# Recurrent mixer of a streaming encoder: gates and convolution weights moved ahead of the receptances, later weight splits moved behind the inverses

## The chip, the cores and the metric

The kernel runs on one core of a Trainium2 chip. The metric is the time of one execution on the device in microseconds. The core's engines are TensorE (PE in the profile: matmuls; its weight loads are PEld), VectorE (DVE), ScalarE (ACT), GpSimd (POOL) and SyncE (SP), which here only starts transfers. Each engine takes its instructions in the order in which they were written into its queue; the queues run side by side and wait for one another by semaphores. DMA transfers are started from SyncE's and ScalarE's queues.

## The reference

Two layers act on a float32 stream x of 256 positions by 1024 channels. Each is a feed-forward network, a mixer and a second feed-forward network, each between two RMS norms. The first layer's mixer is the recurrent one, which the change touches; the second layer's is attention. The recurrent mixer, cut to what matters:

```
proj = h @ w_in                                   # columns: r, k, v, lora (decay, rate, gate), c_val, c_gate
p = p + shift_mu * (previous position of p - p)   # for the recurrent columns
kk = normalised k * k_k;   a = sigmoid(...);   k = k * (1 + (a - 1) * k_a)
# for each of 8 heads of 64 channels, over the positions t:
S_t = S_{t-1} diag(w_t) - (S_{t-1} kk_t)(kk_t * a_t)^T + v_t k_t^T
y_t = S_t r_t
bonus = sum(r * k * r_k) * v                      # over the channels of a head
y_a = (group_norm(y) * lnx_g + lnx_b + bonus) * g
glu = c_val * sigmoid(c_gate)
y_b = silu(layer_norm(conv over 31 positions of glu))
out = concat(y_a, y_b) @ w_out
```

## The kernel before

**Stages.** The kernel runs six stages one after the other: feed-forward 0, recurrent mixer A, feed-forward 1, feed-forward 3, attention mixer C, feed-forward 4. Mixer A takes the stretch from about 207 to 396 us of the span.

**Weights.** Weights come from DRAM in pages of 128 x 1024 fp32, 512 KB each, in one planned list. `Stream.load` starts their loads on SyncE's queue as buffers (`raw`) come free. A page is split before its use: ScalarE casts a high part `whi`, VectorE (for some pages GpSimd) subtracts it and gets the low part `wlo`; TensorE then makes three products (high by high, low by high, high by low). The splits are `split`, line 102 for the cast and 104 for the difference. `upto` splits pages up to a given key. The convolution's pages (`acw`) are used as they come, without a split. Keys: `alora`, `av`, `ak`, `ar` for lora, values, keys and receptances, `acv` and `acg` for the gate values and the gates of the convolution, `ao` for the output.

**Steps of mixer A.** The string `ORDER` names the steps in the order in which they are written out, one letter each. Q (`qmats`) makes for each chunk of 64 positions and each head the matrix that has to be inverted. I (`invert`) writes Q to DRAM (`dq`), reads its 16 x 16 diagonal blocks back (`inv<-dq`), inverts them on VectorE in a chain of small products and sums (lines 774 to 798), writes the inverses to DRAM twice, plain (`dg`) and transposed (`dt`), and reads them back as diagonal blocks of `G` and `T`. R (`receptance`) makes r and its scaled form in `ur`. C (`glu`) makes the gated values of the convolution and shifts them by one position with transfers. A (`amats`) makes the scores of keys and receptances (`ak`, `ar`) in four chunks of 8 products. B (`kback`) transposes keys back and c (`conv`) starts the convolution. 2 (`doubling`) grows the 16 x 16 inverses to 64 x 64 with products of `T`, `Q`, `G` and `WT`. b (`bonus`) makes the bonus on GpSimd. S (`state`) walks the four chunks: Q times G, then `vz`, then the state `SB`. `weigh` makes the weights of the bonus from r times k, 16 small matmuls.

**Taps.** The convolution's 31 taps by channel group are spread as filler: some as scaled additions on VectorE (`feed`, in amounts `FEED`), the others as matmuls on TensorE (`pfeed`, in amounts `PFEED`), 8 taps for each `acw` page. In the trace one fp32 matmul of these is two records.

**What sets the order.** The steps are written in the order of `ORDER`; `issue_after(x)` asks that an instruction be put behind x in the engine's queue.

The four writes of `dq` in `invert`, half on each queue:

```
for t in range(2):
    (nc.scalar, nc.sync)[t].dma_start(out=rows64(dq, c)[:, t], in_=Q[zs, t])
```

## Time and profile before

| | us |
|---|---|
| median of 3 runs | 1115.91 (1115.58 to 1116.05) |
| the profiled execution | 1117.59 |
| its span, first to last instruction | 1115.6 |
| TensorE busy | 1083.3 (97%) |
| VectorE busy | 644.4 (58%) |
| ScalarE busy | 545.0 (49%) |
| GpSimd busy | 208.9 (19%) |
| mean granted clock of TensorE | 0.987 |

The profile is of one execution, taken by the hardware profiler; its times are microseconds from the start of the span. The granted clock is the share of full speed that TensorE had. An engine that is not busy waits, and the trace names what ended the wait. Busy time of TensorE includes time at the lower clock, in which the same work takes twice as long.

### The profile page before, as it was taken

Reading aid. Unit: us, or ns where it says so; the run is one execution under the profiler, and the core shown is the slowest. Engines: PE = TensorE matmul, PEld = TensorE weight load, DVE = VectorE, ACT = ScalarE, POOL = GpSimd, SP = SyncE. Lnnn points to the kernel's source line nnn. Section 1 sums busy time; section 2 is a strip of 40 time slices with the busy share of each in tenths; the row PEclk is TensorE's granted clock in tenths of the full one; section 3 lists DMA queues with packets and bytes.
Section 4 is the critical chain, followed back from the end, with each engine's and each line's share of the span. In section 5 each row is a group of like instructions: output and inputs, shape, how many; then the busy total and the mean of one; then the engine's idle time right before and its main releaser. Section 6 shows DMA issues by size and latency. Waiting matters only on the chain.

```text
span 1115.6 us, 17671 instructions
## 1 busy us (share of the span) xinstructions
PE 1083.3 (97%) x7021; PEld 951.6 (85%) x7021; DVE 644.4 (58%) x1050; ACT 545.0 (49%) x876; POOL 208.9 (19%) x155
## 2 busy tenths in 40 slices
PE   7999999999799999999999999999999999999997
PEld 5899998879688789999888999988787778999986
DVE  4565662578755556557545555836657655555822
ACT  7444544574111574446354544635666855444611
POOL 5200004334030160000034000001555423000000
PEclk9999999999699999999999999999999999999999
DMA  9765785246621138655635454744273555665400
GB/s 356 253 215 183 239 292 150 82 157 189 152 86 58 43 147 281 229 174 208 222 116 209 167 188 177 271 159 150 78 273 124 159 177 180 219 181 193 140 1 38
DMA packets 66632, 192.84 MB, mean 173 GB/s; under 512 B 18520, under 2 KB 20216, under 8 KB 66550
## 3 DMA queue, kind: packets, MB, share of 16 engines
q1 hardware_dynamic: 56698, 189.75, 50.2%
q10 hardware_dynamic: 9852, 1.96, 1.0%
q8 instruction: 55, 0.90, 0.3%
q14 instruction: 27, 0.22, 0.1%
HBM read 187.86 MB, written 2.92 MB: 171 GB/s over the span
## 4 chain that ended last, share of the span: by engine, by line
PE 85%; DVE 5%; ACT 4%; issue 2%; DMA 2%; POOL 1%; ACTq 0%; SPq 0%; DVEq 0%; POOLq 0%
PE gu L361 31%; PE acc L270 21%; PE gu L230 15%; PE acc L600 5%; PE gu L347 4%; PE acc L372 3%; PE gu L600 1%; ACT whi L102 1%; DVE wlo L104 1%; DMA inv<-dq 1%; POOL misc L118 1%; POOL p L496 1%; PE tr L250 1%; PE tr L163 1%; DMA raw<-in_wgt_dram 1%
## 5 line engine op out<-in xcount | busy, mean ns | idle before, releaser
L102 ACT CAST whi<-raw 128x1024 fp32r<-128x1024 f32 x294 | 301.7, 1047 | 212.5 <-PE gu L361 93.2
L104 DVE TENSOR_TENSOR wlo<-raw,whi 128x1024 fp32r<-128x1024 f32 x256 | 317.3, 1248 | 150.5 <-ACT whi L102 125.9
L361 PE MATMUL gu<-xth,whi 128*128 128x256 f32 x1104 | 312.7, 283 | 1.4 <-ACT xth L167 1.4
L361 PE MATMUL gu<-xth,wlo 128*128 128x256 f32 x1104 | 312.8, 284 | 0.0
L361 PE MATMUL gu<-xl,whi 128*128 128x256 f32 x1104 | 312.2, 283 | 0.0
L361 PEld LDWEIGHTS gu<-xth,whi 128*128 128x128 f32 x1104 | 211.5, 192 | 5.0 <-ACT xth L167 2.0
L361 PEld LDWEIGHTS gu<-xth,wlo 128*128 128x128 f32 x1104 | 211.6, 192 | 2.6 <-issue 0.3
L361 PEld LDWEIGHTS gu<-xl,whi 128*128 128x128 f32 x1104 | 211.3, 192 | 1.2 <-issue 1.0
L270 PE MATMUL acc<-whi,ht 128*128 128x512 f32 x576 | 168.2, 393 | 0.0
L118 POOL TENSOR_TENSOR misc<-misc 128x1 f32<-128x1 f32 (+1 forms) x36 | 32.3, 898 | 496.5 <-DVE misc L135 377.4
L104 POOL TENSOR_TENSOR wlo<-raw,whi 128x1024 fp32r<-128x1024 f32 x38 | 92.2, 2459 | 157.3 <-PE acc L270 140.6
L270 PEld LDWEIGHTS acc<-whi,ht 128*128 128x128 f32 x576 | 103.9, 189 | 18.2
L270 PE MATMUL acc<-wlo,ht 128*128 128x512 f32 x288 | 89.9, 392 | 0.0
L241 DVE TENSOR_TENSOR h<-gu,h 128x256 f32<-128x256 f32 x88 | 36.8, 419 | 75.5 <-ACT h L237 71.9
L230 PE MATMUL gu<-whi,xth 128*128 128x512 f32 x160 | 63.1, 400 | 2.5 <-ACT whi L102 1.5
L270 PEld LDWEIGHTS acc<-wlo,ht 128*128 128x128 f32 x288 | 53.9, 188 | 11.8
L230 PE MATMUL gu<-wlo,xth 128*128 128x512 f32 x160 | 63.3, 397 | 0.5 <-DVE wlo L104 0.5
L230 PE MATMUL gu<-whi,xl 128*128 128x512 f32 x160 | 63.5, 400 | 0.0
L239 DVE TENSOR_TENSOR h<-gu,misc 128x256 f32<-128x256 f32 x56 | 23.7, 423 | 65.2 <-PE gu L361 65.1
L237 ACT ACTIVATE h<-gu,misc 128x256 f32<-128x256 f32 x32 | 15.1, 474 | 76.1 <-PE gu L230 42.3
L104 POOL TENSOR_TENSOR flo<-raw,fhi 128x1024 fp32r<-128x1024 f32 x8 | 19.0, 2389 | 149.8 <-ACT fhi L102 149.4
L347 PE MATMUL gu<-whi,xth 128*128 128x512 f32 x112 | 44.7, 399 | 1.6 <-ACT v L435 1.6
(259 smaller groups left out, 1528.5 us busy)
## 6 DMA issues: line engine op xcount, KB each, us to landing
raw<-in_wgc_dram SPq DMA_DIRECT2D x112, 512.0 KB, 4.7
raw<-in_wd_dram SPq DMA_DIRECT2D x88, 512.0 KB, 5.0
raw<-in_wgt_dram SPq DMA_DIRECT2D x64, 512.0 KB, 5.5
raw<-in_cin_dram SPq DMA_DIRECT2D x24, 512.0 KB, 4.9
raw<-in_ain_dram SPq DMA_DIRECT2D x18, 512.0 KB, 4.7
raw<-in_aout_dram SPq DMA_DIRECT2D x8, 512.0 KB, 5.8
raw<-in_cgate_dram SPq DMA_DIRECT2D x8, 512.0 KB, 4.5
raw<-in_cout_dram SPq DMA_DIRECT2D x8, 512.0 KB, 5.0
```

Source lines behind the costliest of these rows:

```text
L102: self.nc.scalar.copy(out=hi, in_=raw)
L104: (engine or self.nc.vector).tensor_tensor(out=lo, in0=raw, in1=hi.bitcast(F32), op=ALU.subtract)
L118: self.pow = self.nc.gpsimd.tensor_tensor(out=out, in0=v, in1=self.mhalf[:, :n], op=ALU.pow)
L230: nc.tensor.matmul(ps, lhsT=l, rhs=r[:, k % 2], start=n == 0, stop=n == 23)
L237: nc.scalar.activation(sl, ps[:, 0:256], AF.Silu, scale=rstd[u[2]])
L239: nc.vector.tensor_tensor(out=z, in0=ps[:, 0:256], in1=self.rb, op=ALU.mult)
L241: nc.vector.tensor_tensor(out=h, in0=ps[:, 256:512], in1=sl, op=ALU.mult)
L270: mm = nc.tensor.matmul(out, lhsT=l, rhs=r, start=u[1] == 0 and i + n == 0, stop=u[1] == NB - 1 and i * 3 + n == 5)
L347: self.nc.tensor.matmul(ps, lhsT=l, rhs=r[:, k % 2], start=n == 0, stop=n == 23)
L361: self.nc.tensor.matmul(ps[:, j * 256:(j + 1) * 256], lhsT=l, rhs=r, start=n == 0, stop=n == 23)
L372: yield lambda acc, l=l, r=r, c=c, first=k == ks[0] and n == 0, last=k == ks[7] and n == 2: self.nc.tensor.matmul(acc[c], lhsT=l, rhs=r[:, ...
L600: return nc.tensor.matmul(out, lhsT=lhsT, rhs=rhs, start=start, stop=stop, skip_group_check=True)
```

## The change

The change does these things in mixer A:

- Gates and gate values (C) and the convolution's start (c) are written ahead of the receptances (R); R now makes r times k itself. The weighing matmuls, and a new step p (`ahead`) with the first taps, stand ahead of the scores, and two taps behind each chunk of them. `PFEED` is 16, 2, 2, 6.
- The `acw` pages are loaded ahead of the `ao` pages. The first `ao` load stands behind the first gate shift, the later ones behind the loads of `G` and `T`.
- All four writes of `dq` go through ScalarE's queue; the write of `dg` goes through SyncE's, that of `dt` stays on ScalarE's. The constants of the inverse and its products share one buffer.
- The splits of `ao` and of the next stage are held behind the last `G` of the doubling (`m["doubled"]`) and the last copy of `kback`.
- The norm's gain page (`ln`) takes the buffer of k and is loaded through ScalarE's queue; the output's gain page (`gp`) is fetched 7 weight loads behind and not 14.

```diff
-ORDER = "VLDKPvQskRICABc2bS"
+ORDER = "VLDKPvQskICcRpAB2bS"
...
-FEED, PFEED = (3, 2, 6), (14, 2, 8)
+FEED, PFEED = (3, 2, 6), (16, 2, 2, 6)
...
-                    (nc.scalar, nc.sync)[t].dma_start(out=rows64(dq, c)[:, t], in_=Q[zs, t])
+                    nc.scalar.dma_start(out=rows64(dq, c)[:, t], in_=Q[zs, t])
...
-            for src, dd, dst in ((TI, dt, T), (GV, dg, G)):
-                nc.scalar.dma_start(out=diag(dd), in_=src)
+            for src, dd, dst, queue in ((TI, dt, T, nc.scalar), (GV, dg, G, nc.sync)):
+                queue.dma_start(out=diag(dd), in_=src)
                 for zs, c in halves:
                     for t in range(2):
-                        (nc.scalar, nc.sync)[t].dma_start(out=dst[zs, t], in_=rows64(dd, c)[:, t])
+                        i = (nc.scalar, nc.sync)[t].dma_start(out=dst[zs, t], in_=rows64(dd, c)[:, t])
+
+            W.gates[W.where["ao", 0][1] + 1] = i
...
+            V.tensor_tensor(out=r, in0=r, in1=k, op=ALU.mult)
+
         def weigh(behind):
             rk = grp(m["r"])
+            psb = self.bank("tr", 2)
             with self.tc.issue_after(behind.ins):
-                V.tensor_tensor(out=rk, in0=rk, in1=m["k"], op=ALU.mult)
...
+                        with self.tc.issue_after(m["ahead"].ins):
+                            i = mm(pss[hp][:, g, :], both(bk, g, t, c)[b], both(ur, g, t, c)[b])
+                pfeed(PFEED[1], i)
...
+        def ahead():
             feed(FEED[0])
-            pfeed(PFEED[0])
+            m["ahead"] = pfeed(PFEED[0])
...
-            W.upto(("ao", 1))
-            W.upto(("ao", 0))
+            with self.tc.issue_after(m["doubled"].ins), self.tc.issue_after(m["back"].ins):
+                W.upto(("ao", 1))
+                W.upto(("ao", 0))
...
-        for key in then:
-            W.upto(key)
+        with self.tc.issue_after(m["doubled"].ins), self.tc.issue_after(m["back"].ins):
+            for key in then:
+                W.upto(key)
...
+                for j in range(6):
+                    W.add(("acw",), flat(a["acw"][j]), 128, True)
                 for h in (2, 3, 0, 1):
                     W.add(("ao", h // 2), flat(a["aout"][h]), 1024)
-                for j in range(6):
-                    W.add(("acw",), flat(a["acw"][j]), 128, True)
```

Three places show how the instructions move. First VectorE's queue from the end of the doubling to the first chunk of the state, before the change; `G` is the grown inverse, `glu` a tap, `vz` the first chunk's value:

```order
L957 SCALAR_TENSOR_TENSOR glu<-glu,cst 128x232
L915 TENSOR_TENSOR G<-acc_3281,G 128x512
L957 SCALAR_TENSOR_TENSOR glu<-glu,cst 128x231
L1039 TENSOR_TENSOR vz<-acc_3324,misc 64x512
L957 SCALAR_TENSOR_TENSOR glu<-glu,cst 128x230
```

And the same place of the changed kernel, where `wlo` is the split of an output page:

```order
L967 SCALAR_TENSOR_TENSOR glu<-glu,cst 128x231
L922 TENSOR_TENSOR G<-acc_3245,G 128x512
L105 TENSOR_TENSOR wlo<-raw,whi 128x1024 x3
L967 SCALAR_TENSOR_TENSOR glu<-glu,cst 128x230
L105 TENSOR_TENSOR wlo<-raw,whi 128x1024 x5
L1052 TENSOR_TENSOR vz<-acc_3287,misc 64x512
```

Eight splits of output weights came between the last `G` and `vz`; before, they stood among the steps of the inverse and the scores.

Second, ScalarE's queue around the inverse, before the change; `r` are the receptances' activations, the DMA rows are transfers that wait for what they copy:

```order
L663 ACTIVATE r<-n,misc 128x256 x2
L102 CAST whi<-raw 128x1024
L765 DMA dq<-Q 64x8x64 x2
L102 CAST whi<-raw 128x1024
L771 DMA inv<-dq 128x16x16
L102 CAST whi<-raw 128x1024
L663 ACTIVATE r<-n,misc 128x256 x2
L102 CAST whi<-raw 128x1024 x5
L882 ACT_TABLE_LOAD
L882 ACTIVATE z<-z 128x512
L102 CAST whi<-raw 128x1024
L800 DMA dg<-inv 128x16x16
```

The same engine in the changed kernel, from the read of `dq` on:

```order
L774 DMA inv<-dq 128x16x16
L889 ACT_TABLE_LOAD
L889 ACTIVATE z<-z 128x512
L955 ACTIVATE glu<-glu,cst 128x256
L889 ACTIVATE z<-z 128x512
L802 DMA dt<-inv 128x16x16
L805 DMA G<-dg 64x8x64 x2
L805 DMA T<-dt 64x8x64
L664 ACTIVATE r<-n,misc 128x256 x2
L805 DMA T<-dt 64x8x64
L664 ACTIVATE r<-n,misc 128x256 x2
L980 ACTIVATE cv<-acc_2791,cst 64x256
```

The four `r` activations moved from ahead of the inverse to behind the transfers of its results.

Third, TensorE's queue in the changed kernel behind the last projection of the receptances; `acc_2791` rows are the taps of one `acw` page, `tr<-misc,r` the weighing, `acc_2938` and `acc_2937` the first scores:

```order
L601 MATMUL acc_2791<-glu,raw 128x244
L601 MATMUL acc_2791<-glu,raw 128x242
L601 MATMUL tr<-misc,r 128x2 x8
L866 MATMUL tr<-cst,bk 128x128 x4
L601 MATMUL acc_2791<-glu,raw 128x256
```

Before, the weighing stood behind the first products of the doubling; now it stands ahead of the scores, behind one page of taps.

## Rows read from the trace of the kernel before

**Rows 1.** The page, part 1: busy us (share of the span) x instructions.

```profile
PE 1083.3 (97%) x7021; PEld 951.6 (85%) x7021; DVE 644.4 (58%) x1050; ACT 545.0 (49%) x876; POOL 208.9 (19%) x155
```

**Rows 2.** Waits of TensorE, 207 to 396 us: total, times, longest, in us.

```profile
PE gu L600 <- DVE ak L846: 5.7, 1, 5.7
PE acc L600 <- DVE ur L813: 2.4, 1, 2.4
```

**Rows 3.** Windows: length, busy us per engine (instructions), TensorE's granted clock, DMA share, GB/s.

```profile
264.00:284.00 20.00, 19.64 (x176) 19.30 (x176) 15.90 (x33) 8.37 (x11) 5.46 (x4) 1.00 0.68 222
...
288.00:308.00 20.00, 18.27 (x79) 15.45 (x80) 11.81 (x25) 1.68 (x2) 0.15 (x1) 0.50 0.74 145
...
311.00:315.00 4.00, 4.00 (x16) 3.48 (x16) 0.17 (x1) 0.58 (x1) 3.03 (x3) 0.57 0.10 37
...
359.00:363.00 4.00, 4.00 (x42) 3.88 (x41) 2.54 (x4) 1.09 (x2) 0.00 (x0) 0.57 0.02 4
```

**Rows 4.** Timeline of TensorE: start, us, instruction, records, idle time before and its end.

```profile
246.88 1.44 PE L600 MATMUL acc<-ur,bk 64*64 64x64 f32 x64 [0.24 <-DVE bk L718]
...
282.92 1.16 PE L600 MATMUL acc<-ur,bk 64*128 64x128 f32 x16
289.73 0.44 PE L600 MATMUL gu<-vz,ak 64*64 64x64 f32 x2 [5.65 <-DVE ak L846]
...
338.28 3.63 PE L600 MATMUL acc<-glu,raw 128*128 128x256 f32 x16
341.84 0.69 PE L600 MATMUL acc<-vz,kb 128*64 128x64 f32 x16
```

**Rows 5.** Timeline of VectorE from the splits ahead of Q to the inverse's end.

```profile
249.53 2.35 DVE L104 TENSOR_TENSOR wlo<-raw,whi 128x1024 fp32r<-128x1024 f32 x2
...
255.22 3.14 DVE L755 SCALAR_TENSOR_TENSOR Q<-acc,misc,cst 128x64 f32<-128x64 f32 x16
...
270.45 0.43 DVE L774 TENSOR_TENSOR inv<-inv,c 128x256 f32<-128x256 f32 x1 [3.92 <-DMA inv<-dq]
...
287.90 0.37 DVE L798 COPY inv<-inv 128x256 f32<-128x256 f32 x1
```

**Rows 6.** Timeline of ScalarE (ACTq: its queue), and DMA issues, us to landing.

```profile
262.71 0.40 ACTq L771 DMA_DIRECT2D inv<-dq  x1
...
292.80 1.05 ACT L102 CAST whi<-raw 128x1024 fp32r<-128x1024 f32 x1 [2.54 <-DMA dt<-inv]
...
dg<-inv ACTq DMA_DIRECT2D x1, 128.0 KB, 5.6
dt<-inv ACTq DMA_DIRECT2D x1, 128.0 KB, 4.5
```

**Rows 7.** Timeline of VectorE at the end of the doubling.

```profile
337.95 0.69 DVE L915 TENSOR_TENSOR G<-acc,G 128x512 f32<-128x512 f32 x1
...
339.04 0.69 DVE L1039 TENSOR_TENSOR vz<-acc,misc 64x512 f32<-64x512 f32 x1
```

**Rows 8.** Timeline of ScalarE and VectorE, and one group: the receptances' steps.

```profile
265.19 0.91 ACT L663 ACTIVATE r<-n,misc 128x256 f32<-128x256 f32 x2 [0.93 <-DVE n L660]
...
264.48 0.67 DVE L660 TENSOR_TENSOR n<-gu,misc 128x512 f32<-128x512 f32 x1
...
271.40 0.87 DVE L664 SCALAR_TENSOR_TENSOR r<-n,cst,r 128x255 f32<-128x255 f32 x2
...
272.52 0.76 DVE L813 TENSOR_TENSOR ur<-r,ep 128x256 f32<-128x256 f32 x2
...
L822 DVE TENSOR_TENSOR r<-r,k 128x1024 f32<-128x1024 f32 x1 | 1.2, 1215 | 0.0
```

**Rows 9.** Timeline of ScalarE in the output's products.

```profile
382.99 2.93 ACT L102 CAST whi<-raw 128x1024 fp32r<-128x1024 f32 x3
```

**Rows 10.** Timeline of GpSimd and VectorE ahead of Q.

```profile
231.00 2.37 POOL L104 TENSOR_TENSOR wlo<-raw,whi 128x1024 fp32r<-128x1024 f32 x1 [3.32 <-ACT whi L102]
...
231.34 2.32 DVE L715 SCALAR_TENSOR_TENSOR bk<-k,cst,ic 128x256 f32<-128x256 f32 x1 [2.13 <-ACT ic L679]
```

More of the change, by code (lines that the diff above doesn't have):

```diff
@@ L53, in __init__ @@
         self.plan, self.tiles, self.loads = [], [], []
-        self.where, self.pages = {}, []
+        self.where, self.pages, self.gates = {}, [], {}
     def add(self, key, ap, cols, whole=False):
@@ L69, in load @@
             raw = self.raws.tile([P, 1024], F32, name="raw")
-            self.loads.append(kr.nc.sync.dma_start(out=raw, in_=ap))
+            with kr.tc.issue_after(self.gates[len(self.tiles)].ins) if len(self.tiles) in self.gates else contextlib.nullcontext():
+                self.loads.append(kr.nc.sync.dma_start(out=raw, in_=ap))
             self.tiles.append(raw)
@@ L104, in split, with fetch @@
             (engine or self.nc.vector).tensor_tensor(out=lo, in0=raw, in1=hi.bitcast(F32), op=ALU.subtract)
-    def fetch(self, out, ap):
-        with self.tc.issue_after(self.w.loads[-BACK].ins):
+    def fetch(self, out, ap, back=BACK):
+        with self.tc.issue_after(self.w.loads[-back].ins):
             self.nc.sync.dma_start(out=out, in_=ap)
@@ L188, in gain, with gpost @@
         return self.sp[:, 8 * j + k:8 * j + k + 1]
-    def gpost(self, j):
+    def gpost(self, j, back=BACK):
         j = "0A13C4".index(str(j))
         g = self.page("gp")
-        self.fetch(g, self.a["gpost"][j:j + 1, :].broadcast_to([P, D]))
+        self.fetch(g, self.a["gpost"][j:j + 1, :].broadcast_to([P, D]), back)
         return g
@@ L379, in outproj @@
         accs = [[self.bank(f"acc{t}{c}") for c in range(2)] if t or begun is None else begun[0] for t in range(2)]
-        gp = self.gpost(j)
+        gp = self.gpost(j, BACK if begun is None else BACK // 2)
         for t in range(2):
@@ L687, in keys @@
             W.upto(("ak",))
-            k = m["k"] = grp(self.page("k"))
+            m["kpage"] = self.page("k")
+            k = m["k"] = grp(m["kpage"])
             for h in range(2):
@@ L769, in invert @@
             TI = inv[:, 544:800].rearrange("p (t i) -> p t i", i=16)
-            tmp, X = self.temp("tmp", [512]), inv[:, 800:864]
+            room = self.temp("c16", [1024])
+            c16, tmp, X = room[:, 0:512], room[:, 512:1024], inv[:, 800:864]
             nc.scalar.dma_start(out=QI[:, 0:256].rearrange("p (i t) -> p i t", t=16), in_=diag(dq))
-            c16 = self.temp("c16", [512])
             self.fetch(c16, a["c16"])
@@ L817, in receptance @@
                             in1=self.sel.unsqueeze(1).unsqueeze(1).broadcast_to([P, 4, 4, 2]), op=ALU.mult)
+            V.tensor_tensor(out=r, in0=r, in1=k, op=ALU.mult)
         def weigh(behind):
             rk = grp(m["r"])
+            psb = self.bank("tr", 2)
             with self.tc.issue_after(behind.ins):
-                V.tensor_tensor(out=rk, in0=rk, in1=m["k"], op=ALU.mult)
-            psb = self.bank("tr", 2)
-            for t in range(2):
-                for g in range(4):
-                    o = t * 8 + 2 * g
-                    mm(psb[:, o:o + 2], rk[:, g, t * P:(t + 1) * P], selr[:, g, :])
+                for t in range(2):
+                    for g in range(4):
+                        o = t * 8 + 2 * g
+                        mm(psb[:, o:o + 2], rk[:, g, t * P:(t + 1) * P], selr[:, g, :])
             bo = m["bo"] = self.small("bo", 16, 1)
@@ L842, in amats @@
                         b = slice(64 * hp, 64 * hp + 64)
-                        i = mm(pss[hp][:, g, :], both(bk, g, t, c)[b], both(ur, g, t, c)[b])
+                        with self.tc.issue_after(m["ahead"].ins):
+                            i = mm(pss[hp][:, g, :], both(bk, g, t, c)[b], both(ur, g, t, c)[b])
+                pfeed(PFEED[1], i)
                 u, r = (slice(64 * z, 64 * z + 64) for z in (1 - c, c))
@@ L859, in kback @@
                     nc.tensor.transpose(out=tp[:, g * P:(g + 1) * P], in_=both(m["bk"], g, t, c), identity=self.ident)
-                nc.scalar.copy(out=kb[t][:, c, :], in_=tp)
+                m["back"] = nc.scalar.copy(out=kb[t][:, c, :], in_=tp)
         def glu():
@@ L889, in glu @@
                     m["gated"] = V.tensor_tensor(out=gl[i][o, gs, :], in0=cv[o, gs, :], in1=z[o, gs.start - 2 * h:2], op=ALU.mult)
-                    nc.sync.dma_start(out=gl[i][l, gs, 1:256], in_=gl[i][o, gs, 0:255])
+                    W.gates[W.where["ao", 1][0]] = nc.sync.dma_start(out=gl[i][l, gs, 1:256], in_=gl[i][o, gs, 0:255])
         def doubling():
@@ L924, in bonus @@
             bo, gg = m["bo"], m["gg"]
-            ln = half(self.page("ln"))
-            self.fetch(ln.rearrange("p a b -> p (a b)"), a["arow"][0:1, 512:1536].broadcast_to([P, 1024]))
+            ln = half(m["kpage"])
+            with self.tc.issue_after(m["back"].ins):
+                nc.scalar.dma_start(out=m["kpage"], in_=a["arow"][0:1, 512:1536].broadcast_to([P, 1024]))
             Wg = m["Wg"] = half(m["r"])
-            with self.tc.issue_after(m["doubled"].ins):
+            with self.tc.issue_after(m["doubled"].ins), self.tc.issue_after(m["back"].ins):
                 for t in range(2):
@@ L959, in pfeed @@
         def pfeed(n, behind=None):
+            i = behind
             for j, s, w in itertools.islice(m.get("ptaps", iter(())), n):
@@ L970, in pfeed @@
                     V.tensor_copy(out=z[64:P, 16:256], in_=o[64:P, 0:240])
+            return i
         def conv_norm(t):
@@ L1040, in state @@
                 if ch < 2:
[L1041 removed]
+                    pfeed(PFEED[3], i)
                 else:
@@ L1080, in mixer_a @@
         f = {"V": values, "v": lambda: m["rest"](), "s": lambda: m["shift"](), "L": lora, "K": keys, "D": decay, "P": prep, "k": kprep, "Q": qmats, "I": invert, "R": receptance, "A": amats,
-             "B": kback, "C": glu, "2": doubling, "b": bonus, "c": conv, "S": state}
+             "B": kback, "C": glu, "p": ahead, "2": doubling, "b": bonus, "c": conv, "S": state}
         for z in ORDER:
             f[z]()
-        for key in then:
-            W.upto(key)
+        with self.tc.issue_after(m["doubled"].ins), self.tc.issue_after(m["back"].ins):
+            for key in then:
+                W.upto(key)
         ofeed(99, m["last"])
```

5 lines of the change are left out of this document (2 added, 3 removed).

## Prediction

> **What bounds the kernel now.** First the page: TensorE is busy 1083.3 of 1115.6 us [rows 1], so a change can win only what TensorE loses to idling and to its clock, or pay by adding to either. The profiled execution took 1117.59 us beside a span of 1115.6; the runs' median, 1115.91, is 1.7 below it. The sum counts microseconds of that span and is put on the median.
>
> Next, who TensorE waits for between 207 and 396 us, the mixer's stretch. Two waits stand out: 5.7 us for the first `ak` of VectorE, in one piece, and 2.4 us for the receptances' `ur` [rows 2]. Then the same stretch by granted clock. Ahead of the long wait it is 1.00, then 0.50 (1.2 of 2.4 GHz) from 288 to 308 us, though TensorE works for 18.27 of them; shorter falls (0.57 and 0.57 over 4 us each) come later [rows 3]. 18.27 us of work at half speed cost about 9.1 us; each short fall, 3.4 us at half speed within its 4 us window, about 1.7. So the wait before 289.73 [rows 4] costs 5.65 + 9.1 = 14.8 us. The 2.4 us wait brought no fall.
>
> Third, why VectorE was late there: it had the inverse from 270.45, when its input landed, to the copy at 287.90, with weight splits of 1.2 us among its steps, and the `ak` came behind that [rows 5]. What matters for the change is therefore whether TensorE still empties before VectorE delivers, and whether splits that leave this place stall another.
>
> **The change part by part.**
>
> *Q and the inverse.* Ahead of Q's matmuls TensorE now gets 200 of the 128x256 matmuls in place of 176. A window of 20 us held 176 matmuls in 19.64 us, of which 32 were the scores' at 1.16 per 16 [rows 3, 4], so one costs (19.64 - 2.3)/144 = 0.12. The 24 shift Q's start from 246.88 [rows 4] to at most 249.8; I take 249.0, since the order leaves out the short waits just ahead of it. Q's matmuls end 1.4 later, at 250.4. VectorE's Q took 3.14 us and ended at 258.36 [rows 5]. It can't end before 253.5, and it needn't end later than before; I take 254.4, because the receptances' part and several splits no longer stand ahead. From Q's end to the issue of `inv<-dq` it took 262.71 - 258.36 = 4.35 [rows 5, 6]; all four writes on ScalarE's queue, two waiting behind a cast, may cost as much as the two queues before. Landing took 270.45 - 262.71 = 7.7, with weight loads on the queues; the like-sized `dg` took 5.6 and `dt` 4.5 [rows 6]. At 5.6 the inverse starts at 264.4 (bounds from 4.5 to 7.7).
>
> The inverse lasted 17.45 us to its last copy. Six splits (6 x 1.15, two of them taking 2.35 in a row [rows 5]) go, the receptances' 0.87 and 0.76 [rows 8] go, three taps and a gate come for two products of the gate values, under 1 us more: rounded up 10 us, to 274.4. `dg`'s write moves to SyncE's queue behind two gate shifts, which wait for gates made before the inverse's last steps; it costs nothing. SyncE's half of `T` waits behind four `ao` loads, but doubling needs it only past 300 us.
>
> *The receptances.* Here the gain is handed back. The four `r` activations and their VectorE steps now stand behind the inverse on VectorE, and on ScalarE behind the loads `G<-dg` and `T<-dt`. The trace shows that such a load holds ScalarE: the cast behind it sat idle for 2.54 us until `dt` had landed at 292.80 [rows 6]. So `r` begins at 274.7 + 4.5 = 279.2, five microseconds behind the inverse's end. Then come, one behind another in halves, 0.91 of ScalarE per half partly overlapped, 0.87, 0.76, 0.67 of `n`, the second half, and r*k of 1.2 [rows 8]: 6.2 us, to 285.5. r*k was hidden before; now the 16 weighing matmuls wait for it, and behind them everything on TensorE.
>
> TensorE has for this time 232 projection matmuls (27.8) and one page of taps, which took 3.63 [rows 4]: 250.4 + 27.8 + 3.6 = 281.8. So it idles some 4 us, not 5.65, and resumes at 285.5 and not 289.73: **-4.2**. Its bounds are 283.4 (Q at 253.5, transfers at their quickest) and 291.5 (Q's end as before, landing 7.7). By then it has done one tap page more, and the first 32 matmuls of the scores fewer: 3.6 - 2.3 = **-1.3**.
>
> I take it that the clock falls as before, since 4 us lies nearer to 5.65 than to 2.4, and lasts as long: no change, except that the short fall at 311 us is swallowed: **-1.7**. The scores get three banks in place of four: **+0.5** (0 to 1.2, the 16 matmuls of one chunk [rows 4]). `acw` ahead of `ao` and the gate on the `ao` loads cost nothing: those weights aren't split before 300 us, they have over 10 us to land in. Moving `ln` and `gp` likewise ends on GpSimd, off the path.
>
> *The splits behind the doubling.* All eight `ao` splits now stand on VectorE between the last `G` and the state's first `vz`, as the order rows show. Before, that place held one tap: `G` at 337.95, `vz` at 339.04 [rows 7]. At 1.15 apiece eight make 9.2. TensorE's cover there is Q,G and taps: from 338.28 eight taps took 3.63, and `vz,kb` came at 341.84 [rows 4], 2.1 us after `vz` was ready at 339.73. The new order leaves four taps, 1.8 us less cover. Thus 9.2 - 2.1 + 1.8 = **+8.9** of idle TensorE. Bounds: 7 (splits catch up a little) to 10.
>
> That is longer than the 5.65 us wait, which began at 284.08; the clock was down from 288, 4 us into it, for 20 us [rows 3]. The same again leaves 20 - (8.9 - 4) = 15.1 us of work at half speed: **+7.5**, from which the short fall at 359 us [rows 3] is taken, **-1.7**. The least it could cost is 1.7, as there.
>
> *Next stage.* Its splits wait too. Four casts now stand on ScalarE ahead of the last output cast, 3 took 2.93 us [rows 9], and TensorE has little else in the order: **+1.5** (0 to 5).
>
> Sum: -4.2 - 1.3 - 1.7 + 0.5 + 8.9 + 7.5 - 1.7 + 1.5 = **+9.5 us**, so 1115.9 + 9.5 = **1125.4 us**.
>
> On the clock the Trainium skill speaks differently (TensorE: Matmul & The Clock Gate, What's actually happening): a busy TensorE gets its full clock back soon, not after 20 us. The trace disagrees, with 18.27 busy us at 0.50; by the page the second fall would cost little more than the short one, which is the second rival below.
>
> **The rivals.**
>
> First, the clock holds through the receptances' gap. It takes idling that stays nearer 2.4 than 5.65, that is `r*k` by about 284.5. Then 9.1 us of the old loss are won: +0.4, **1116.3 us**, no change. For it: TensorE's new tap page and Q's lead. Against it: the transfer and the ScalarE hold, which can hardly shrink below 4.5.
>
> Second, the clock comes back quickly behind the splits, as at 359 us, costing 1.7 where 7.5 stands: +3.7, **1119.6**. For it: a short fall did so. Against it: the only long idle time did not.
>
> Third, and on the other side, both at once: 9.5 - 9.1 - 5.8 = -5.4, **1110.5**, faster. One mechanism decides it, the clock's answer to gaps of 4 and 9 us; the point is whether the first stays under some 3 us. A close relative is that the splits hold TensorE less than bounded, worth up to 3 more.
>
> Fourth, GpSimd delays the inverse. At 231.00 a GpSimd split of 2.37 us began and the VectorE step at 231.34 took 2.32, as long as the split [rows 10]. The receptances' four splits move on GpSimd to where VectorE makes Q and the inverse; two such meetings cost some 4, with the gap growing to 8 to 9: about +14, **1130**.
>
> The Trainium skill has the reason (SBUF — State Buffer, SBUF: two separate sides): a shared port pair that one holds for a whole instruction. The trace agrees with it at 231 us; if every one of the four met a step, the sum would be higher by about 8.
>
> **How the numbers follow.** Chances: the forecast 0.42; first rival 0.22; second 0.10; third with its relative 0.21; fourth 0.05. The forecast's own range is 1120 to 1131 from its bounds. The range for all, 1109 to 1131, reaches from the third rival to the fourth. About 0.2% (2.2 us) is what a measurement can tell from no change. Faster: the third and a third of the first, 0.28; same: the rest of the first and little else, 0.14; slower: 0.58.
>
> **What would show it.** Right: in the changed profile a wait of TensorE for `r` of about 4 us at 282 to 286; clock 0.50 for some 20 us behind it; eight splits in one row on VectorE, a wait for `vz` of 8 to 9 us, and a second 0.50 stretch. Q should end near 254, the inverse near 274. Wrong: clock 1.00 over the scores and taps (first or third rival), a `vz` wait under 6 us, or the inverse's input landing later than 267.

## The result, and the profile after

The changed kernel takes **1123.64 us** (median of 4 runs, 1123.48 to 1125.12), the kernel before 1115.74 beside it (4 runs, 1113.41 to 1116.05): a ratio of 1.0078, 95% interval 1.0061 to 1.0096, slower. Forecast were 1125.4 us. The profiled execution has a span of 1121.6 us, 6.0 more than before. The profile of the kernel before is one of its longer executions: 38 that were timed beside the runs below had spans of 1111.0 to 1116.7 us, half of them under 1113.7, at mean granted clocks of 0.986 to 0.991. So the two profiles differ by less than the medians do (6.0 against 7.9 us).

TensorE has as much work as before (the ledger below) and is idle for longer. The page, part 1, of the changed kernel [rows 1]:

```profile
PE 1078.3 (96%) x7018; PEld 947.2 (84%) x7021; DVE 650.5 (58%) x1050; ACT 544.3 (49%) x876; POOL 207.6 (19%) x155
```

Its waits from 205 to 440 us [rows 2]: the pieces of 5.7 and 2.4 us are gone, two longer ones have come, both on VectorE.

```profile
PE acc L601 <- DVE vz L1052: 8.9, 3, 7.9
PE tr L601 <- DVE r L823: 6.9, 1, 6.9
PE acc L373 <- ACT xth L103: 2.0, 1, 2.0
...
PE acc L373 <- DVE xl L105: 0.9, 1, 0.9
```

TensorE's timeline around them [rows 4]. The first tap page is done ahead of the first hole; TensorE resumes at 290.71, a microsecond later than before.

```profile
280.28 3.52 PE L601 MATMUL acc<-glu,raw 128*128 128x256 f32 x16
290.71 3.55 PE L601 MATMUL tr<-misc,r 128*128 128x2 f32 x16 [6.91 <-DVE r L823]
...
334.94 1.92 PE L601 MATMUL acc<-glu,raw 128*128 128x248 f32 x8
344.78 1.12 PE L601 MATMUL acc<-vz,kb 128*64 128x64 f32 x16 [7.92 <-DVE vz L1052]
```

VectorE's timeline [rows 5, 7]: Q, the inverse from first step to last copy, r*k, and then the last `G`, eight splits in two groups, and the state's first `vz`.

```profile
256.19 3.15 DVE L757 SCALAR_TENSOR_TENSOR Q<-acc,misc,cst 128x64 f32<-128x64 f32 x16
...
266.64 0.43 DVE L776 TENSOR_TENSOR inv<-inv,c 128x256 f32<-128x256 f32 x1 [2.55 <-DMA inv<-dq]
...
268.28 2.35 DVE L792 TENSOR_TENSOR c<-inv 128x16 f32<-128x16 f32 x2
...
280.07 0.40 DVE L800 COPY inv<-inv 128x256 f32<-128x256 f32 x1
...
289.34 1.23 DVE L823 TENSOR_TENSOR r<-r,k 128x1024 f32<-128x1024 f32 x1
...
333.87 0.68 DVE L922 TENSOR_TENSOR G<-acc,G 128x512 f32<-128x512 f32 x1
334.47 3.48 DVE L105 TENSOR_TENSOR wlo<-raw,whi 128x1024 fp32r<-128x1024 f32 x3
337.87 0.45 DVE L967 SCALAR_TENSOR_TENSOR glu<-glu,cst 128x230 f32<-128x230 f32 x1
338.24 5.76 DVE L105 TENSOR_TENSOR wlo<-raw,whi 128x1024 fp32r<-128x1024 f32 x5
344.03 0.69 DVE L1052 TENSOR_TENSOR vz<-acc,misc 64x512 f32<-64x512 f32 x1
```

The last `G` comes 4.1 us earlier than before (333.87, not 337.95), and the first `vz` 5.0 us later (344.03, not 339.04).

Windows of the changed kernel (columns as in [rows 3]):

```profile
282.00:300.00 18.00, 11.09 (x53) 9.73 (x53) 6.12 (x13) 3.11 (x7) 2.41 (x5) 0.72 0.96 252
300.00:334.00 34.00, 33.75 (x478) 27.35 (x477) 23.84 (x52) 10.93 (x15) 7.40 (x6) 1.00 0.27 92
334.00:352.00 18.00, 9.94 (x97) 8.64 (x97) 14.84 (x20) 1.64 (x3) 0.00 (x0) 0.81 0.64 210
352.00:390.00 38.00, 33.80 (x274) 28.04 (x273) 17.83 (x29) 13.67 (x24) 4.40 (x4) 0.96 0.16 56
390.00:440.00 50.00, 48.83 (x250) 41.23 (x251) 32.27 (x53) 29.95 (x57) 23.20 (x12) 0.97 0.45 158
```

**A ledger.** From such windows, cut to one microsecond, two sums can be made for any stretch: TensorE's idle time (length less busy time) and what it loses to the clock (busy time x (1 - granted clock)). Taken from the whole span they leave the work at full clock. It is 1070.0 to 1072.5 us in every kernel of this study, so the two sums account for the differences to within 2.5 us. Each row is one execution. Idle + lost to the clock, us:

| kernel | span | 205-282 | 282-300 | 300-334 | 334-352 | 352-390 | 390-440 | rest | left |
|---|---|---|---|---|---|---|---|---|---|
| before | 1115.6 | 4.5+0 | 5.7+5.1 | 0+5.7 | 0.1+0 | 2.5+1.7 | 0+0 | 19.4+0 | 1070.8 |
| changed | 1121.6 | 1.4+0 | 6.9+3.2 | 0.2+0 | 8.1+1.8 | 4.2+1.7 | 1.2+1.7 | 21.4+0 | 1070.0 |
| splits in chunks | 1125.6 | 1.4+0 | 7.0+3.6 | 5.2+2.3 | 0.7+0 | 4.1+1.6 | 3.6+3.0 | 20.9+1.7 | 1070.6 |
| splits unheld | 1124.3 | 1.4+0 | 15.9+0.6 | 2.4+5.0 | 1.7+0 | 2.0+0 | 3.0+1.7 | 20.0+0 | 1070.6 |
| ar splits on VectorE | 1128.8 | 3.2+0 | 8.9+2.7 | 1.8+0.7 | 5.7+1.7 | 1.6+1.7 | 4.0+1.7 | 20.8+1.7 | 1072.5 |
| queues as before | 1120.9 | 1.4+0 | 6.9+3.5 | 0.2+0 | 8.1+1.9 | 4.5+1.7 | 0.9+1.7 | 20.1+0 | 1070.1 |
| receptances early | 1125.1 | 2.0+1.7 | 8.7+1.7 | 0+0 | 7.9+1.6 | 2.3+2.8 | 3.2+1.5 | 21.3+0 | 1070.3 |
| splits, two places | 1122.4 | 1.4+0 | 13.6+1.6 | 0.9+2.4 | 0+0 | 2.0+1.7 | 3.7+2.9 | 19.9+1.7 | 1070.6 |
| both of these | 1122.4 | 2.1+0 | 9.8+1.7 | 2.5+1.6 | 1.0+0 | 4.6+1.3 | 3.8+3.4 | 20.4+0 | 1070.4 |
| taps into the hole | 1118.8 | 1.4+0 | 6.9+3.5 | 0.6+0 | 7.3+2.0 | 4.2+0.1 | 0+1.5 | 20.7+0 | 1070.6 |
| splits spread | 1114.0 | 1.4+0 | 6.9+3.1 | 0+0 | 0.1+0 | 6.5+2.0 | 0+1.2 | 21.1+1.7 | 1070.1 |
| splits on GpSimd | 1123.5 | 1.4+0 | 6.8+4.2 | 3.6+2.9 | 1.4+0 | 3.8+1.3 | 3.4+2.0 | 19.8+1.6 | 1071.3 |
| spread, and tail | 1107.1 | 1.4+0 | 7.0+4.1 | 0.2+0 | 0.1+0 | 2.2+0 | 0+0 | 21.3+0 | 1070.9 |
| and reads on SyncE | 1104.2 | 1.3+0 | 5.0+3.4 | 0.3+0 | 0.1+0 | 2.2+0 | 0+0 | 20.5+0 | 1071.4 |

Before against changed: the stretch up to 334 us is 9.3 us cheaper (21.0 to 11.7), the state's start 9.8 dearer (0.1 to 9.9), what follows up to 440 us 4.5 dearer (4.2 to 8.7). With 1.9 more in the other stretches and 0.8 less of work that is the difference of 6.0, but for rounding.

### The profile page after: what moved, and what is told of

It is laid out like the page before. It is cut to its first block, busy times and chain, and to the rows that moved or that the text cites. A ratio compares the mean times of both kernels' runs of the same rounds, so it can differ in the third digit from the quotient of the medians.

```text
span 1121.6 us, 17676 instructions
## 1 busy us (share of the span) xinstructions
PE 1078.3 (96%) x7018; PEld 947.2 (84%) x7021; DVE 650.5 (58%) x1050; ACT 544.3 (49%) x876; POOL 207.6 (19%) x155
## 4 chain that ended last, share of the span: by engine, by line
PE 85%; DVE 8%; ACT 3%; issue 2%; DMA 1%; POOL 1%; ACTq 0%; SPq 0%; DVEq 0%; POOLq 0%
PE gu L362 32%; PE acc L271 21%; PE gu L231 15%; PE gu L348 5%; PE acc L373 4%; PE acc L601 3%; DVE wlo L105 2%; PE gu L601 1%; POOL misc L119 1%; DVE glu L967 1%; DMA raw<-in_wgt_dram 1%; POOL p L497 1%; PE tr L251 1%; PE tr L601 1%; PE tr L164 1%
## 5 line engine op out<-in xcount | busy, mean ns | idle before, releaser
L271 PEld LDWEIGHTS acc<-whi,ht 128*128 128x128 f32 x576 | 103.9, 189 | 18.3
L231 PE MATMUL gu<-whi,xth 128*128 128x512 f32 x160 | 63.3, 398 | 3.8 <-ACT whi L103 2.7
L241 ACT ACTIVATE h<-h 128x256 f32<-128x256 f32 x56 | 23.2, 415 | 73.2 <-DVE h L240 73.2
```

The source lines that it names most:

```text
L231: nc.tensor.matmul(ps, lhsT=l, rhs=r[:, k % 2], start=n == 0, stop=n == 23)
L241: nc.scalar.activation(sl, z, AF.Silu)
L271: mm = nc.tensor.matmul(out, lhsT=l, rhs=r, start=u[1] == 0 and i + n == 0, stop=u[1] == NB - 1 and i * 3 + n == 5)
```

## The experiments

All start from the changed kernel unless it is said. The **theory**: the block of splits ahead of the first `vz` costs its length and its half clock (9.9 us in the ledger), the receptances behind the inverse the other hole (10.1). The **equal-cost rival**: the splits cost the same wherever VectorE does them. Issue order is asked for by `issue_after`, which binds only instructions on the engine of the instruction named; that matters below. In the diffs `m["rk"]` is r*k's instruction, `("mask", n)` the last mask of chunk n and `"masked"` that of the last chunk, `("SB", n)` the state's S product of chunk n, `"lasty"` and `"lastcast"` the split and cast of the output's last operand.

**1. The splits among the masks.**

```
-            with self.tc.issue_after(m["doubled"].ins), self.tc.issue_after(m["back"].ins):
+            with self.tc.issue_after(m["back"].ins):
                 W.upto(("ao", 1)); W.upto(("ao", 0))
```

> Edit: the eight output-weight splits wait for the last transposed b*k copy alone, no longer for the doubling, so VectorE does them among the a-matrix masks (300 to 316 us of the changed kernel's trace, where VectorE is busy 8.4 of 15 us) instead of in one block between the last G and the state's first v-z product. Theory (the block costs what the trace shows at the state's start): TensorE's wait of 7.9 us there goes to under 1.5 us, the half-clock stretch of 6.8 us behind it goes too (3.4 us of work), and the span falls from 1121.6 to 1108 to 1112 us, about 1110 to 1113 as a median. Rival (9.2 us of splits cost the same wherever VectorE does them): TensorE now waits 5 to 9 us for the masks' banks between 300 and 316 us, and the time stays between 1119 and 1125 us.

1127.69 us (ratio to before 1.0105, 1.009 to 1.012): the rival's side, and above its range. The state's hole did go (8.1 to 0.7 us), but the splits stood three, two, two and one between the masks. VectorE's timeline of this run:

```profile
306.29 3.49 DVE L105 TENSOR_TENSOR wlo<-raw,whi 128x1024 fp32r<-128x1024 f32 x3
...
311.02 2.34 DVE L105 TENSOR_TENSOR wlo<-raw,whi 128x1024 fp32r<-128x1024 f32 x2
...
314.18 3.61 DVE L105 TENSOR_TENSOR wlo<-raw,whi 128x1024 fp32r<-128x1024 f32 x2
...
318.60 1.39 DVE L105 TENSOR_TENSOR wlo<-raw,whi 128x1024 fp32r<-128x1024 f32 x1
320.02 0.41 DVE L981 COPY cv<-acc 64x240 f32<-64x240 f32 x1
320.46 0.69 DVE L916 TENSOR_TENSOR WT<-acc,cst 128x512 f32<-128x512 f32 x1
```

The first `WT` came at 320.46 where the changed kernel has it at 313.63, and TensorE waited 5.0 us ahead of it. My count of idle microseconds there was right, 6.6 of 15 (300 to 315 us), but eight splits of 1.15 need 9.2, and the last three took 5.0 beside GpSimd's steps of the bonus.

**2. The splits without a hold.** The same lines with no `with` at all.

> Edit: the hold on the eight output-weight splits is taken away altogether. In VectorE's order they then stand among the second half of the receptances and ahead of r*k, and their loads are only issued from 284.75 us on. Theory (where they stand decides): the hole at the state's start is gone (-11 us with its half clock), but the receptances now wait for the landings (about 7 us each, the third one ahead of r*k), so that TensorE's hole at 283.8 us grows from 6.9 to some 12 to 16 us, with more half clock behind it: 1116 to 1124 us, slower than the run with the splits among the masks by 5 us or more. Rival (any place but the block will do): 1109 to 1113 us, as fast as that run. Rival (the splits cost the same everywhere): 1121 to 1125 us, with a hole of 8 us that is new and none at the receptances.

1126.15 us (1.0096, 1.0081 to 1.0111); the hole at the receptances grew to 15.9 us, as the theory said, the rest was dearer than its range. The splits wait in VectorE's order for casts that wait for loads:

```profile
291.91 1.23 DVE L105 TENSOR_TENSOR wlo<-raw,whi 128x1024 fp32r<-128x1024 f32 x1 [6.39 <-ACT whi L103]
...
296.25 1.22 DVE L105 TENSOR_TENSOR wlo<-raw,whi 128x1024 fp32r<-128x1024 f32 x1
297.38 1.22 DVE L823 TENSOR_TENSOR r<-r,k 128x1024 f32<-128x1024 f32 x1
```

So in this order a hold is needed, and none of the three places so far (the block, among the masks, without a hold) is good. That it was slower than run 1 by 5 us fell: it was 1.5 faster.

**3. The receptances' splits on VectorE.**

```
-POOLED = ("alora", "ar", "av", "d0", "d1", "g1", "gate0")
+POOLED = ("alora", "av", "d0", "d1", "g1", "gate0")
```

> Edit: the four splits of the receptances' weights go from GpSimd to VectorE. Theory (GpSimd's splits hold VectorE's instructions that run beside them): beside them the b*k products took 3.97 us for two, two steps of the inverse 1.15 and 2.35 us; without them these take about 2.4, 0.45 and 0.5 us, while VectorE gets four splits of 1.2 us, two ahead of Q and two in its idle stretch from 259 to 266 us. Q ends 0 to 1 us later, the inverse needs 2 to 3 us less, r*k ends 1.5 to 3 us earlier, and TensorE's wait for it falls from 6.9 to 4 to 5.5 us: 1119.5 to 1122.5 us. Rival (VectorE is short of time there, and its own 4.9 us more count): r*k ends 1 to 4 us later, TensorE waits 8 to 11 us: 1125 to 1129 us.

1129.07 us (1.0118, 1.0101 to 1.0135): in time the rival. The two inverse steps that took 2.35 us beside a GpSimd split took 0.27, so the hold by GpSimd is real; but VectorE's own splits made Q end at 261.3 us, not 259.3, and the inverse's copy came at 281.25, not 280.07. Even so the receptances' first half began at 282.26, 2.2 us earlier than in the changed kernel. What was not foreseen held their second half: three output loads were issued ahead of `dt`'s write, which landed in 8.6 us and not 3.2, and `T`'s reads wait for it in ScalarE's order. From SyncE's timeline, the DMA issues and ScalarE's timeline:

```profile
280.12 1.50 SPq L71 DMA_DIRECT2D raw<-in_aout_dram  x3
...
dt<-inv ACTq DMA_DIRECT2D x1, 128.0 KB, 8.6
...
290.37 0.65 ACTq L805 DMA_DIRECT2D T<-dt  x1
291.07 0.51 ACT L664 ACTIVATE r<-n,misc 128x256 f32<-128x256 f32 x1 [7.90 <-issue]
```

So this run does not show by itself what these splits cost the kernel on either engine.

**4. The queues as before.**

```
-                    nc.scalar.dma_start(out=rows64(dq, c)[:, t], in_=Q[zs, t])
+                    (nc.scalar, nc.sync)[t].dma_start(out=rows64(dq, c)[:, t], in_=Q[zs, t])
-            for src, dd, dst, queue in ((TI, dt, T, nc.scalar),(GV, dg, G, nc.sync)):
+            for src, dd, dst, queue in ((TI, dt, T, nc.scalar),(GV, dg, G, nc.scalar)):
```

> Edit: Q's four writes go through two queues again as before the change, and the inverse's second write through ScalarE's queue. No engine's compute order changes. Theory (the short landings of 2.9 to 3.2 us, against 4.5 to 7.7 us before, come from the weight loads that now wait behind the inverses, not from the queues): the landings stay under 3.6 us, the inverse starts within 1 us of 266.6 us, and the time is within 2 us of the changed kernel's 1123.6. Rival (the queues make them): the landing of Q's blocks goes back to 5 us or more, the inverse and TensorE's resumption come 2 to 5 us later, and the time rises to 1126 to 1130 us.

1122.4 us, as the theory said. Landings were 2.8 (`inv<-dq`), 3.1 (`dg`) and 3.3 us (`dt`), in the changed kernel 2.9, 3.1 and 3.2. So the queues are worth nothing that can be told apart (ratios to before of 1.0057, 1.004 to 1.0073, and 1.0078, 1.0061 to 1.0096), and they don't make the landings short. Weight loads just ahead make them long, as two runs with the queues of the change show: `dt`'s 8.6 us behind three loads in run 3, and 7.2 us for `inv<-dq` behind three loads in run 5 (issued at 265.14, first inverse step at 272.35).

**5. The receptances ahead of the inverse.**

```
-ORDER = "VLDKPvQskICcRpAB2bS"
+ORDER = "VLDKPvQskRICcpAB2bS"
```

> Edit: in the order of the steps the receptances stand again ahead of the inverse (as before the change); all other parts of the change stay, the hold on the eight splits too. Theory (holes are set by what stands in VectorE's order, and the one at 283.8 us by the receptances behind the inverse): with r*k done ahead of the inverse, TensorE goes from the taps straight into the a-matrices, so that the wait of 6.9 us and its half-clock stretch (10.2 us, 5.1 us of work) go, the wait of 2.4 us for u*r at 262 us comes back, and the state's hole of 7.9 us stays: 1121.6 - 12.0 + 2.4 = 1112 us (1109 to 1115). Rival (the hole only moves on, as the run with the splits among the masks has shown for the other one): T's landing or the masks hold TensorE for 5 us or more at the doubling, 1118 to 1123 us.

1127.02 us (1.0089, 1.0074 to 1.0104): above both ranges. The hole moved on, as the rival says, but to another place than it names. The wait for r*k went, and TensorE's next instruction waited instead, the first taps, for the shift of the gates, which now stand behind the inverse on VectorE. The waits of this run:

```profile
PE acc L601 <- DVE vz L1052: 9.7, 3, 7.9
PE acc L601 <- DMA glu<-glu: 8.6, 1, 8.6
```

Gates, taps and receptances compete for one stretch of VectorE, and in the orders run here what came last made a hole of 7 to 10 us. How much of this hole is VectorE's order is not shown, since the inverse also started 5.7 us later than in the changed kernel, 4.3 of it by the landing of `inv<-dq` (7.2 us, not 2.9).

**6. The splits in two places**, and **7. both**.

```
+            with self.tc.issue_after(m["rk"].ins):            # 7: m["masked"], and run 5's ORDER
+                W.upto(("ao", 1))
 ...
                 if ch == 2:
                     ofeed(OFEED[1], m["last"])
+                    with self.tc.issue_after(m["SB", 2].ins):
+                        W.upto(("ao", 0))
```

> Edit: the first four output-weight splits stand right behind r*k, where VectorE was idle for some 9 us (291 to 300 us), the last four behind the third chunk's S product (from 366 us on), where its idle shares are above half; ScalarE's casts of the two groups go with them. Theory (splits cost nothing where VectorE is idle and its next instruction is not waited for): the hole of 7.9 us and its half clock (3.4 us) go, the masks and the doubling start when they did: 1121.6 - 11.3 = 1110 us, with up to 3 us back where the last four run (the state's last products, or loads of the next weights, which wait for the same buffers): 1109 to 1114 us. Rival (the time is conserved: what the state gains, the next stage's start waits for): 1119 to 1125 us.

> Edit: receptances ahead of the inverse again, and the eight splits in two places (four behind the last mask, four behind the third chunk's S product). Theory: both savings of the changed kernel's two holes add, 1121.6 - 9.6 - 11.3 = 1101 us, less sure by what the splits behind the masks do to the doubling's first product (up to 4.6 us) and its clock: 1100 to 1108 us, faster than the kernel before by 0.8% or more. Rival (each hole moves on to the next place where VectorE is late): 1112 to 1118 us, no faster than the kernel before.

1122.41 us (1.0053, 1.0038 to 1.0068) and 1124.77 (1.0077, 1.0062 to 1.0092). Run 6 is not the test that its text describes: the holds name VectorE's instructions, so that ScalarE's casts went free. ScalarE's timeline shows two of them waiting for loads ahead of the receptances' second half:

```profile
291.19 1.04 ACT L103 CAST whi<-raw 128x1024 fp32r<-128x1024 f32 x1 [6.21 <-DMA raw<-in_aout_dram]
292.45 1.04 ACT L103 CAST whi<-raw 128x1024 fp32r<-128x1024 f32 x1 [0.21 <-DMA raw<-in_aout_dram]
293.40 0.90 ACT L664 ACTIVATE r<-n,misc 128x256 f32<-128x256 f32 x2
```

The hole there grew from 6.9 to 13.6 us and ate what the state gave (334 to 352 us: 9.9 to 0). In run 7 the taps' wait for the gates (9.6 us) came with run 5's order. Both missed the theory's range, and run 7 the rival's as well. Run 6 lies in its rival's range, and a part of "time is conserved" did happen, 6.6 us lost where the next stage starts and not 2.9 (390 to 440 us); but most of what came back is the new cause, the casts.

**8. Taps into the hole.**

```
-FEED, PFEED = (3, 2, 6), (16, 2, 2, 6)
+FEED, PFEED = (3, 2, 6), (16, 2, 1, 14)
```

> Edit: one tap less behind each of the ten matrix products of the doubling and ten more in the state's first chunk, that is, ten taps of about 0.24 us each in TensorE's hole of 7.9 us. Theory (the hole is idle time that any ready work fills): TensorE's wait falls to 5 to 6 us, the doubling ends 1 to 2.4 us earlier, and the time is 1 to 3 us less, 1118.5 to 1121 us by the span. Rival (the doubling waits for VectorE as soon as its taps are gone): new waits of 2 us or more there, and the time within 0.5 us of 1121.6 or above.

1121.33 us by the median, 1118.8 by the span, 2.8 less: the theory's range, but not for its reason. The wait hardly shrank; the doubling, ten taps shorter, ended 3.5 us earlier (last `G` at 330.35), and the block with it. By the ledger only 0.6 us of the gain lie at the state's start (9.9 to 9.3) and 2.9 behind it (352 to 440 us, 8.7 to 5.8), which the theory did not speak of:

```profile
330.89 2.77 PE L601 MATMUL acc<-glu,raw 128*128 128x252 f32 x12
341.27 1.12 PE L601 MATMUL acc<-vz,kb 128*64 128x64 f32 x16 [7.61 <-DVE vz L1052]
```

**9. The splits spread**, ScalarE's casts held as in the changed kernel.

```
+            for n, z in zip(W.where["ao", 1], (("mask", 0), ("mask", 1), ("mask", 2), ("mask", 3))):
+                with self.tc.issue_after(m[z].ins), self.tc.issue_after(m["back"].ins):
+                    W.page(n)
 ...            # and in the state, after its third chunk's last products:
+                    for n, z in zip(W.where["ao", 0], (("SB", 0), ("SB", 0), ("SB", 1), ("SB", 2))):
```

> Edit: of the eight output-weight splits the first four wait one each for the last mask of a chunk of the a-matrices, the last four stand behind the S products of the state's first three chunks (two, one, one); ScalarE's casts stay behind the last b*k copy, as in the changed kernel (the run with two places had set them free, and two of them, waiting for their loads, stood ahead of the receptances). Theory (a split is free where VectorE's next instruction is not yet ready, and costs its full length where it is): the receptances' hole stays 6.9 us, the state's 8.1 + 1.8 us go to 1 us or less, and 0 to 2.5 us come at the doubling's start: 1121.6 - 9 + 0 to 2.5 = 1112.5 to 1115.5 us, at or just below the kernel before. Rival (the doubling's start waits as long as with all eight among the masks, 5.2 + 2.3 us): 1120 to 1122 us.

1115.91 us, ratio 1.0004 (0.9994 to 1.0013): level with the kernel before, 7.6 us of span below the changed one. The state's hole is gone (8.1 + 1.8 to 0.1), no new one stands before it (300 to 334 us: 0), the receptances' is 6.9 as before. VectorE reaches the first `vz` right behind the doubling:

```profile
333.36 0.69 DVE L923 TENSOR_TENSOR G<-acc,G 128x512 f32<-128x512 f32 x1
...
334.93 0.70 DVE L1053 TENSOR_TENSOR vz<-acc,misc 64x512 f32<-64x512 f32 x1
```

This settles the main point: the same eight splits, on the same engine, cost 9.8 us in one place and at most 1.0 in others (352 to 440 us: 8.7 to 9.7); the equal-cost rival falls, and runs 1 and 2 were two more bad places. The 1.7 in the rest is a fall of the clock at 805 us, in a stage that the change doesn't touch. Idle time is left behind the state, 6.5 us. VectorE there:

```profile
372.82 4.63 DVE L105 TENSOR_TENSOR wlo<-raw,whi 128x1024 fp32r<-128x1024 f32 x4 [2.03 <-ACT whi L103]
377.49 0.69 DVE L105 TENSOR_TENSOR xl<-tr,xth 128x512 fp32r<-128x512 f32 x1
381.03 1.29 DVE L133 TENSOR_TENSOR f<-acc,gp 128x512 f32<-128x512 f32 x2 [2.86 <-DMA gp<-in_gpost_dram]
```

Four splits for the next stage stand ahead of the output's last operand, and the gain row lands late.

**10. The splits on GpSimd** (`"ao1", "ao0"` added to `POOLED`, casts held by `m["back"]`).

> Edit: the eight output-weight splits go to GpSimd, ScalarE's casts stay behind the last b*k copy. Theory: VectorE has no block left, so the state's hole of 8.1 + 1.8 us goes; but eight GpSimd splits of 2.4 to 2.8 us run beside the masks and the doubling, and each holds a VectorE instruction as the inverse's and the b*k products were held (1 to 1.9 us each): with half of them meeting one that TensorE waits for, 4 to 6 us come back there, 1115 to 1118 us. Rival (GpSimd's work is free): 1111 to 1113 us. Rival (every split holds VectorE for its whole length): 1121 us or more, with TensorE's waits in the doubling above 10 us.

1124.96 us (1.0083, 1.006 to 1.0106), span 1123.5: slower than the theory, nearer the last rival, though TensorE's waits in the doubling stayed far below 10 us (300 to 334 us: 3.6 + 2.9). Where the hold strikes is plain in VectorE's timeline:

```profile
318.12 4.45 DVE L967 SCALAR_TENSOR_TENSOR glu<-glu,cst 128x250 f32<-128x250 f32 x2
...
326.74 6.70 DVE L967 SCALAR_TENSOR_TENSOR glu<-glu,cst 128x247 f32<-128x247 f32 x5
333.47 0.69 DVE L922 TENSOR_TENSOR G<-acc,G 128x512 f32<-128x512 f32 x1
```

The two taps at 318.12, beside four GpSimd splits in a row (312.47 to 322.30), took 0.97 us in run 9. The five at 326.74 took 2.51 there; here they ran beside one split and steps of the bonus that the splits had pushed back. `G`, which reads a bank of PSUM, took its usual 0.69, and the masks theirs.

**11. Run 9 and the tail; 12. and the reads on SyncE.**

```
-        gp = self.gpost(j, BACK if begun is None else BACK // 2)
+        gp = self.gpost(j, BACK)
-        with self.tc.issue_after(m["doubled"].ins), self.tc.issue_after(m["back"].ins):
+        with self.tc.issue_after(m["lasty"].ins), self.tc.issue_after(m["lastcast"].ins):
             for key in then: W.upto(key)
# 12 as well:
-                        i = (nc.scalar, nc.sync)[t].dma_start(out=dst[zs, t], in_=rows64(dd, c)[:, t])
+                        i = nc.sync.dma_start(out=dst[zs, t], in_=rows64(dd, c)[:, t])
```

> Edit, on top of the run with the spread splits: the casts and splits of the next stage's first weights stand behind the last cast and split of the output's operand, and the gain row of the output is loaded seven loads earlier. Theory (TensorE's waits at the stage's end come from what stands ahead in ScalarE's and VectorE's order, and from a late gain row): of the 6.5 us of idle and 3.2 us of half clock between 352 and 440 us in the run before this one, the 2.9 us of wait for the last operand and the 2.9 us that VectorE waits for the gain row go, with half of the half clock: 1114.0 - 3 to 6 = 1108 to 1111 us by the span, 0.3 to 0.6% below the kernel before. Rival (the next stage's first products then wait for their own weights, 4.6 us of splits later): 1113 us or more, with a new wait of 2 to 5 us at the next stage's first matmul.

> Edit, on top of that: the reads of G and T all go through SyncE's queue, so that none stands in ScalarE's order. Theory (ScalarE's first receptance activation, ready at 282.6 us, ran at 284.5 us because the read of T ahead of it waited for its write to land): r*k ends 1.5 to 2 us earlier, TensorE's hole falls from 6.9 to about 5 us and its half clock with it: 1.5 to 3 us less than the run without this edit. Rival (the activation waits for VectorE, or T's and G's reads one after the other on one queue come later, and the doubling waits for them): no gain, within 0.5 us, or 1 to 3 us more with a wait for T at the doubling.

1108.94 us (0.9942, 0.9929 to 0.9954) and **1106.76 us** (0.9927, 0.9914 to 0.9941): both theories held, and both runs are faster than both kernels, the last by 0.7% against the kernel before. Run 11's span, 1107.1, is a microsecond below its range; the tail's 9.7 us (352 to 440) fell to 2.2, of which the rival's wait for the next stage's own weights is 1.8. In run 12 ScalarE runs the first receptance activation at 282.21, in the changed kernel at 284.49 behind a read that waited for `dt`; the hole is 5.0 us. ScalarE in the changed kernel, then in run 12:

```profile
283.85 0.59 ACTq L805 DMA_DIRECT2D T<-dt  x1
284.49 0.51 ACT L664 ACTIVATE r<-n,misc 128x256 f32<-128x256 f32 x1 [4.05 <-POOL glu L979]
...
282.21 0.91 ACT L664 ACTIVATE r<-n,misc 128x256 f32<-128x256 f32 x2 [2.18 <-DVE n L661]
```

TensorE's waits and two windows of run 12:

```profile
PE tr L601 <- DVE r L823: 5.0, 1, 5.0
PE gu L231 <- POOL wlo L105: 1.8, 1, 1.8
```

```profile
282.00:300.00 18.00, 12.98 (x72) 11.39 (x72) 7.45 (x18) 3.23 (x7) 2.26 (x4) 0.81 0.99 245
...
334.00:352.00 18.00, 17.91 (x225) 15.15 (x223) 15.19 (x27) 6.22 (x11) 2.75 (x3) 1.00 0.39 118
```

## Why the prediction was right, and where its terms were off

**Both causes were right; the clock and the end of the first hole were not.** Slower, because the splits that the change takes out of the inverse stand ahead of the first `vz`, and because the receptances' part behind the inverse hands the early gain back. Run 9 shows the first, run 12 the second: 2.3 us off the chain of the receptances took 1.9 off the hole. The forecast of 1125.4 us lies 1.8 above the median, and that is in part luck, since errors cancelled. Its sum, by stretch, is -6.7 us up to 334 us, +16.4 at the state's start and -0.2 behind it; the profiles show -9.3, +9.8 and +4.5, and +1.1 elsewhere. Of its own signs the eight splits and a wait for `vz` came (7.9 us, just under its 8 to 9); the hole ahead of the weighing was 6.9 us and not 4, both half-clock stretches were shorter than its 20 us, and the inverse's input landed 0.4 us ahead of the 267 that it had named as a sign of being wrong.

**"TensorE resumes at 285.5: -4.2"** was off by 5 us: it resumed at 290.71. Two steps failed. *Q ending at 254.4*: it ended at 259.34 (before 258.36). TensorE came to Q's products only at 251.25, past the bound of 249.8, VectorE still had splits ahead of Q, and its two `b*k` products took 3.97 us beside a GpSimd split, 2.88 in run 3, without splits but beside other GpSimd steps, and 1.35 before. *The inverse in 10 us*: it took 13.8 (266.64 to 280.47), 2.8 of it beside GpSimd: two steps took 2.35 us beside a split (0.27 in run 3), and one 1.15 beside GpSimd's step for the values, not a split as run 3's text has it (0.42 in run 5, with GpSimd idle). That is in part the mechanism of the prediction's fourth rival, to which 0.05 was given. In its favour the landings were shorter (2.9 for `inv<-dq` and 3.2 for `dt`, not 5.6 and 4.5). The chain behind was sized well: 6.1 us from the first `r` to the end of r*k, where 6.2 to 6.3 stood. The Trainium skill's rule on the port pair (SBUF — State Buffer, SBUF: two separate sides: GpSimd and a VectorE instruction with two SBUF inputs exclude each other for a whole instruction) agrees with run 10: taps stretched (two from 0.97 to 4.45 us), instructions with a PSUM input not (`G`, 0.69).

**"The clock falls as before and lasts as long"** was wrong, and its error went the other way. By one-microsecond windows, twice the sum of (1 - clock) gives the length of a half-clock stretch: 20.5 us before, 10.2 in the changed kernel, of which TensorE worked only from 290.71 on. Up to 334 us the clock cost 3.2 us and not 10.8; with the short fall at 311 gone as forecast, that is 7.6 won where 1.7 stood. The prediction read its 20 us from one execution, and the kernel before does not always lose that much: from a mean clock of 0.987, as profiled, to the 0.991 of some other executions is, by an estimate of twice 0.004 x 1115, some 9 us less at half clock.

**"+8.9 of idle TensorE"** at the splits: 8.0 (8.1 against 0.1), with a wait of 7.92 in one piece. The block of 9.2 us on VectorE was right to a tenth.

**"+7.5" for the second fall** was mis-sized most: 6.8 us of half clock, and 1.8 us lost. Here the prediction's second rival is what happened. The Trainium skill (TensorE: Matmul & The Clock Gate, What's actually happening: activity releases the throttle) was the better guide for this fall, which took 6.8 us, and the trace of before, with 18.3 us of half-clock work, the worse. Why that one lasted so long stays open; stretches of like length came only in run 2 (20.5 us) and run 6 (17.1 us), where TensorE was idle for most of them.

**"-1.7" for the short fall at 359 us** did not come: a like fall stood at 365 us. The **"+0.5"** for the scores' banks was at most 0.2, the idle time from 300 to 334 us.

**"+1.5" for the next stage** was 4.5 (from 352 us on, 4.2 to 8.7): the casts and splits for the next stage held the last operand (waits of 2.0 and 0.9 us), and one fall of the clock came behind these waits (392 to 397 us, 1.7 us lost). Run 11, on top of run 9, shows that they were the cause, together with the gain row, since both edits together took 7.5 us out; which of the two gave how much was not run apart.

## What to carry to other kernels

Moving work off one stretch of a busy engine isn't a gain until it is known what waits where it goes: list the idle time of that engine by stretch, cut the moved block so that each piece fits into one, and hold each piece behind the instruction after which there is room. An order request must be given for every engine that the work uses, or its other half (here ScalarE's casts and their loads) moves ahead of what it should follow. Keep a ledger of idle time and clock losses of the bounding engine by stretch: its remainder stayed within 2.5 us over fourteen kernels, so that every edit could be read as gains and losses with a place.
